# Two-branch attention: the scan or normalisation emitted one step later, PSUM copies assigned to an engine by branch, bias tiles in a pool of their own

## The chip, the cores and the metric

The kernel runs on one NeuronCore of a Trainium2 chip. Five engines have instruction queues of their own, which run in order and wait for one another on semaphores: TensorE (PE in the profile, with PEld for its weight loads), VectorE (DVE), ScalarE (ACT), GpSimd (POOL) and SyncE (SP), which here issues nearly all DMAs. TensorE writes its results to PSUM; VectorE or ScalarE copies them from there to SBUF. The metric is the device time of one execution in microseconds; the kernel before takes 1027.94 us, the median of three runs (1027.63, 1027.94, 1033.99).

## The reference

One step of a hybrid streaming encoder layer: 1024 prompt tokens and 64 sample tokens with a cache of 512, model width 1024, all in fp32. One input projection gives two attention branches of 8 heads of 64, which are gated, projected, merged, projected again and added to the input.

```python
def stick_breaking(q, k, v, q_pos, k_pos):            # branch "sb"
    z = einsum(q, k) * ATTN_SCALE
    log_keep = where(causal, log_sigmoid(-z), 0.0)
    suffix = cumsum(log_keep, reverse=True) - log_keep
    w = where(causal, exp(log_sigmoid(z) + suffix), 0.0)
    return einsum(w, v)

def band_attention(q, k, v, q_pos, k_pos, rel_bias):  # branch "cb"
    s = einsum(q, k) * ATTN_SCALE + rel_bias[clip(q_pos - k_pos)]
    return einsum(softmax(where(k_pos >= 0, s, NEG_INF)), v)
```

## The kernel before

The kernel first makes the input projection with an algorithm that saves a part of the products (up to about 500 us of the trace), then the attention (about 503 to 885 us), then the merge and the output projection. The change lies in the attention.

The attention is one loop over a list `seq` of 136 steps. A step is a branch b, a pair of heads p (four in each branch), a block of queries t and a head hd of the pair. The whole sb branch runs first, then cb. Within a pair the sample block t = 8 comes first, with both heads in one step, then t = 0 to 7 with two steps each; so a pair has 17 steps. A step has n keys: in sb n = 128(t+1), up to 1024; in cb at most 640; for t = 8, 576.

The framework is told to keep the order in which the program emits instructions (`manual_schedule`), so the order of each engine's queue is the order of the text. One pass of the loop, for step i, emits in turn:

- `qk(i)` (L1010): TensorE makes the scores z. In sb ScalarE takes two sigmoids of z, into `kp` and `be` (L1037, L1038), and POOL sets one column of `kp`. In cb VectorE adds the bias, takes the minimum as it goes (L1040), and ScalarE takes the exponential with its sum (L1044).
- `prefetch` and `load_z`: DMAs on SP for the steps and pairs to come, and `flush`, which issues the stores held back from the pass before.
- `fill`: matmuls of other work that is independent of the attention (the rest of the gate projection, then the projection of the sb branch, L781 and L881), half of the step's portion.
- `av` (L1106): when a block of queries is complete, weights times values (L1125) into one PSUM buffer `o`, and on VectorE the product with the gate (L1130), which frees that buffer.
- `tr(i-3)` (L1065): TensorE transposes the weights of the step three before (L1086), in groups of at most four blocks, into one of two PSUM buffers `pt`; each group is then copied to SBUF (L1095 on ScalarE or L1097 on VectorE). A third group can't be transposed before the first has been copied.
- `mid(i)` (L1047): in sb VectorE scans `kp` (L1054) and multiplies `be` by it (L1055). In cb VectorE takes the reciprocal of the sum (L1057) and ScalarE scales `be` (L1058). `mid` has neither matmuls nor DMAs.
- the other half of `fill`.

The copies are shared out by a counter `flip`, one count for each group. Before the change, in sb three of four go to ScalarE and every fourth to VectorE; in cb they alternate.

The bias tiles of cb, two of 128x640 and one (`bsm`) for the sample block for each pair, are loaded by `load_bias` (L1158): DMAs on SP, then two small memsets on POOL. They lie in the pool `ay`, which is opened at the first step of cb after the sb pool `axs`, with `kp` and the scan's constants, is closed; `ay` takes the space that `axs` had, and it later holds other tiles (`ot`) too. The tiles of the other cb pairs are loaded one pair ahead.

Of the kernel before, what the change touches and what calls it, by code (L numbers as in the profile page):

```python
# [8 lines left out]
F32 = mybir.dt.float32  # L9
# [23 lines left out]
def hybrid_step_kernel(ctx: ExitStack, tc: tile.TileContext, x_prompt, x_sample, c_sbk, c_sbv, c_cbk, c_cbv,  # L33
# [164 lines left out]
    with ExitStack() as ph:  # L198
# [251 lines left out]
        for i in range(nb):  # L450
            for ti, t in enumerate(TO):
# [38 lines left out]
                if ti in (3, 6) and i > 0 or ti in (5, 6) and i == 0:  # L490
                    h = 1 if ti == 6 else 0
# [37 lines left out]
                if (i, ti) in ((1, 1), (1, 5)):  # L529
                    for s in range(2):  # L530
                        h = ti // 4
# [131 lines left out]
    att = ExitStack()  # L663
# [4 lines left out]
    psZ = att.enter_context(tc.tile_pool(name="az", bufs=3, space=PS))  # L668
    psT = att.enter_context(tc.tile_pool(name="at", bufs=2, space=PS))
    psO = att.enter_context(tc.tile_pool(name="ao", bufs=1, space=PS))  # L670
    sbx = ExitStack()
    ax = sbx.enter_context(tc.tile_pool(name="axs", bufs=2))

# [10 lines left out]
    def flush(every=False):  # L684
        todo = deferred[:]
        deferred.clear()
        for n, f in todo:
            if n <= 0 or every:
                f()
            else:  # L690
                deferred.append((n - 1, f))
# [18 lines left out]
    SQ, KS, VP, BI, st, wT, zts = {}, {}, {}, {}, {}, {}, {}  # L710
# [50 lines left out]
    late = {}  # L761
# [224 lines left out]
    def fill(n):  # L986
        n += owed[0]
        owed[0] = 0
        while n > 0:
# [9 lines left out]
    seq = [(b, p, t, hd) for b in ("sb", "cb") for p in range(NPAIR) for t in [8] + list(range(8))  # L999
           for hd in range(2) if t < 8 or hd == 0]  # L1000

    def band(b, t):
        if t == 8:
            return 0, 576
        if b == "sb":
            return 0, (t + 1) * 128
        k0 = max(0, t - 4)
        return k0, (t + 1 - k0) * 128

    def qk(i):  # L1010
        b, p, t, hd = seq[i]
        key = (b, p)
        r = 128
        k0, n = band(b, t)
        hs = [(0, n)] if n <= 512 else [(0, n // 2), (n // 2, n)]
        be = am.tile([128, NP], F32, name="be", bufs=4)
        if t == 8:
            s, ks, q0 = SQ[key, 3], KS[key, 1], 0
        else:
            s, ks, q0 = SQ[key, t // 3], KS[key, 0], (t % 3) * 128  # L1020
        if b == "sb":
            kp = ax.tile([128, NP + 2], F32, name="kp", bufs=3)
            G.memset(kp[:r, n:n + 1], 0.0)
        else:
            kp = am.tile([128, 4], F32, name="sm", bufs=6)
            bt = BI[2 * p + hd] if t < 8 else BI["s", p]
            off = 0 if t == 8 else 640 - n
        for j, (x, y) in enumerate(hs):
            z = psZ.tile([128, 512], F32, name="z")
            o = k0 * 128  # L1030
            m = y - x
            parts = [(2 * h + e, h) for h in ((0, 1) if t == 8 else (hd,)) for e in range(2)]
            for e, h in parts:
                TE.matmul(z[:, :m], s[:, e, q0:q0 + 128], ks[:, h, o + x:o + y], start=e == parts[0][0],  # L1034
                          stop=e == parts[-1][0])
            if b == "sb":
                A.activation(kp[:r, x:y], z[:r, :m], AF.Sigmoid, scale=-0.125)  # L1037
                A.activation(be[:r, x:y], z[:r, :m], AF.Sigmoid, scale=0.125)  # L1038
            else:
                V.tensor_tensor_reduce(be[:r, x:y], z[:r, :m], bt[:r, off + x:off + y], 1.0,  # L1040
                                       BIG if j == 0 else kp[:r, j - 1:j], OP.add, OP.min, kp[:r, j:j + 1])
        if b == "cb":
            j = len(hs) - 1
            A.activation(be[:r, :n], be[:r, :n], AF.Exp, bias=kp[:r, j:j + 1], scale=-1.0, accum_out=kp[:r, 2:3])  # L1044
        st[i] = (be, kp)

    def mid(i):  # L1047
        b, p, t, hd = seq[i]
        r = 128
        k0, n = band(b, t)  # L1050
        be, kp = st[i]
        if b == "sb":
            im = ims[:] if t == 8 else imp[:, NP - n:NP]
            V.tensor_tensor_scan(kp[:r, n - 1::-1], kp[:r, n - 1::-1], im[:, ::-1], 0.0, op0=OP.mult, op1=OP.add)  # L1054
            V.tensor_tensor(out=be[:r, :n], in0=be[:r, :n], in1=kp[:r, 1:n + 1], op=OP.mult)  # L1055
        else:
            V.reciprocal(kp[:r, 3:4], kp[:r, 2:3])  # L1057
            A.activation(be[:r, :n], be[:r, :n], AF.Copy, scale=kp[:r, 3:4])  # L1058

    def wbase(b, j):  # L1060
        return max(0, 2 * j - 4) if b == "cb" and j < 4 else 0

    flip = [0]

    def tr(i):  # L1065
        b, p, t, hd = seq[i]
        r = 128
        k0, n = band(b, t)
        be, _ = st.pop(i)
        j = t // 2 if t < 8 else 4  # L1070
        q0 = (t % 2) * 128 if t < 8 else 0
        s0 = k0 - wbase(b, j)
        nblk = (n + 127) // 128
        groups = {}
        for kb in range(nblk):
            groups.setdefault((s0 + kb) // 4, []).append(kb)
        for g, kbs in groups.items():
            wk = (b, p, j, hd, g)
            if wk not in wT:
                wT[wk] = ak.tile([128, 4, 256], F32, name="wT", bufs=4)  # L1080
            w = wT[wk]
            pt = psT.tile([128, 4, 128], F32, name="pt")
            kr = 128
            for x, kb in enumerate(kbs):
                kr = min(128, n - kb * 128)
                TE.transpose(pt[:kr, x, :r], be[:r, kb * 128:kb * 128 + kr], ident[:r, :r])  # L1086
            m = len(kbs)
            sl = (s0 + kbs[0]) % 4
            if kr < 128:
                m -= 1  # L1090
                A.activation(w[:kr, sl + m, q0:q0 + r], pt[:kr, m, :r], AF.Copy)
            if m:
                flip[0] += 1
                if flip[0] % 2 or b == "sb" and flip[0] % 4:
                    A.activation(w[:, sl:sl + m, q0:q0 + r], pt[:, :m, :r], AF.Copy)  # L1095
                else:
                    V.tensor_copy(w[:, sl:sl + m, q0:q0 + r], pt[:, :m, :r])  # L1097


    def load_z(b, p, j):  # L1100
        zt = am.tile([128, 256], F32, name="zt", bufs=3)
        nq = 256 if j < 4 else 64
        SP.dma_start(zt[:, :nq], d_z[b][p][:, 256 * j:256 * j + nq])
        zts[b, p, j] = zt
# [51 lines left out]
            load_bias(2 * np_ + 1)  # L1156

    def load_bias(h):  # L1158
        bt = late["y"].tile([128, 640], F32, name="bias", bufs=4)
        src = d_rb[h][0:1, 127:128]  # L1160
        SP.dma_start(bt, bass.AP(tensor=src.tensor, offset=src.offset, ap=[[767, 128], [1, 640]]))
        G.memset(bt[0:64, 576:640], BIG)
        G.memset(bt[64:128, 0:64], BIG)
        BI[h] = bt
        if h % 2:
            bs = BI["s", h // 2] = late["y"].tile([128, 576], F32, name="bsm", bufs=2)
            for w in range(2):
                src = d_rb[h - 1 + w][0:1, 127:128]
                SP.dma_start(bs[64 * w:64 * w + 64], bass.AP(tensor=src.tensor, offset=src.offset,
                                                             ap=[[767, 64], [1, 576]]))  # L1170
# [16 lines left out]
    for i in range(len(seq) + LAG + 1):  # L1187
        m = 0
        if i < len(seq):
            b, p, t, hd = seq[i]  # L1190
            if b == "cb" and p == 0 and t == 8 and hd == 0:
                sbx.close()
                yst = ExitStack()
                late["y"] = yst.enter_context(tc.tile_pool(name="ay", bufs=2))
                load_bias(0)
                load_bias(1)
            qk(i)
            if hd == 0:
                if t % 2 == 1 or t == 8 and (b, p) != ("sb", 0):
                    load_z(b, p, t // 2 if t < 8 else 4)  # L1200
                prefetch(b, p, t)
            acc += amount[b] * wt[b](band(b, t)[1]) / tot[b]
            if (b, p, t) == ("cb", 0, 8):
                acc += 12
            m = int(acc) - emitted
            emitted += m
        flush()
        if i < len(seq) and seq[i][:3] == ("cb", 0, 1) and hd == 1:
            late["sb"] = True
        fill(m // 2)  # L1210
        while avq:
            av(*avq.pop(0))
        if 0 <= i - LAG < len(seq):
            tr(i - LAG)
            b, p, t, hd = seq[i - LAG]
            if t == 8 or hd == 1 and t % 2 == 1:
                avq.append((b, p, t // 2 if t < 8 else 4))
        if i < len(seq):
            mid(i)
        fill(m - m // 2)  # L1220
    flush(True)
    yst.close()
# [177 lines left out]
    for i in range(2):  # L1400
# [3 lines left out]
        for q, s in enumerate(OP_):  # L1404
# [14 lines left out]
            for c in range(2) if s != "b" else ():  # L1419
# [9 lines left out]
                p = ps[:]  # L1429
# [15 lines left out]
                if s in (3, 4, 5, 6):  # L1445
                    w, half = {3: (0, 0), 4: (1, 1), 5: (1, 0), 6: (0, 1)}[s]
                    ys.append(ys.pop(0))
                    y = ys[-1]
                    x = {3: xrs.pop((i, w, half, c)) if s == 3 else None, 4: None, 5: s1[c], 6: u2[c]}[s]
                    if s == 4:  # L1450
                        p, x = u3[c], xrs.pop((i, 1, 1, c))
# [61 lines left out]
```

## Time and profile before

| | |
|---|---|
| median of the three runs | 1027.94 us |
| the profiled execution's own time | 1032.53 us |
| its span on the page | 1030.8 us |
| PE busy over the span | 981.3 us (95%) |
| DVE, ACT, POOL busy | 636.9, 514.3, 345.9 us |
| DVE busy in the sb attention (503 to 697 us) | 164.75 of 194 us |
| ACT busy there | 126.37 of 194 us |

The profile is of one execution. A row of a window view gives its length and the busy time of each engine with its number of instructions, then the clock granted to TensorE (1.00 is full speed), the share of the DMA engines and their rate. A row of groups gives line, engine and operation, the shapes, the count, the busy time and the mean duration in ns, then the idle time just before them and what ended it. A row of waits gives who waited for whom, with total, number and longest wait in us. In a timeline a row gives start and duration, and the idle time of that engine before it in square brackets.

### The profile page before, as it was taken

The page shows a single profiled execution, that of the slowest core. Times are in us where ns is not written, and L with a number is a line of the kernel's source. Part 1 is how long each engine was busy: PE and PEld are TensorE (multiplying, and loading weights), DVE is VectorE, ACT ScalarE, POOL GpSimd, SP SyncE. Part 2 cuts the span into 40 slices and gives each one's busy share as a digit, 9 for nine tenths or more (in the row PEclk, how much of TensorE's full clock was granted, in tenths as well). Part 3 has the DMA queues.
Part 4 walks back from the last instruction along what each step waited for, and adds up shares of the span by engine and source line. Part 5 has one row for each costly group of instructions (what it writes and reads, how often), then busy time and mean ns, then how long its engine had stood idle before and what let it go on. Part 6 is the DMA issues. An engine that isn't in the chain of part 4 may idle for free.

```text
span 1030.8 us, 20364 instructions
## 1 busy us (share of the span) xinstructions
PE 981.3 (95%) x7568; PEld 925.4 (90%) x7568; DVE 636.9 (62%) x1188; ACT 514.3 (50%) x1142; POOL 345.9 (34%) x356
## 2 busy tenths in 40 slices
PE   6999999999999999999999989896899999799998
PEld 5999999999999999999987868785778887799998
DVE  5466673985545565332298969793665764489745
ACT  5534442444344333332385757574777866355320
POOL 3376662124544454442111011010201100377452
PEclk9999999999999999999999989998999999999999
DMA  7636468344663433332985556446888872773642
GB/s 240 207 133 209 164 223 300 115 125 146 185 187 119 126 113 99 92 110 87 240 213 151 150 134 164 113 125 173 236 223 239 246 220 67 233 222 100 190 124 95
DMA packets 177412, 171.04 MB, mean 166 GB/s; under 512 B 35040, under 2 KB 163168, under 8 KB 177184
## 3 DMA queue, kind: packets, MB, share of 16 engines
q1 hardware_dynamic: 168592, 161.41, 53.0%
q10 hardware_dynamic: 8720, 8.33, 2.6%
q8 instruction: 60, 0.98, 0.4%
q14 instruction: 40, 0.33, 0.1%
HBM read 110.96 MB, written 58.72 MB: 165 GB/s over the span
## 4 chain that ended last, share of the span: by engine, by line
PE 78%; DVE 9%; ACT 4%; DMA 4%; issue 2%; SPq 1%; POOL 0%; DVEq 0%; ACTq 0%
PE b L634 24%; PE acc L464 19%; PE b L1427 7%; PE o L1125 6%; PE acc L781 5%; PE b L925 5%; PE pt L1086 4%; DVE kp L1054 4%; PE z L1034 3%; PE acc L881 2%; DVE be L1055 2%; ACT be L1044 2%; DVE be L1040 1%; DVE wT L1097 1%; ACT wT L1095 1%
## 5 line engine op out<-in xcount | busy, mean ns | idle before, releaser
L1086 PE MATMUL pt<-ident,be 128*128 128x128 f32 (+1 forms) x568 | 92.8, 287 | 24.1 <-DVE wT L1097 12.7
L1086 PEld LDWEIGHTS pt<-ident,be 128*128 128x128 f32 (+1 forms) x568 | 67.8, 144 | 38.8 <-DVE wT L1097 16.2
L122 POOL TENSOR_TENSOR wlo<-wraw,whi 128x1024 fp32r<-128x1024 f32 x22 | 55.4, 2519 | 118.0 <-ACT whi L115 117.8
L1054 DVE TENSOR_TENSOR_SCAN kp<-kp,imp 128x128 f32<-128x128 f32 (+7 forms) x64 | 90.4, 1412 | 0.3 <-ACT kp L1037 0.3
L1034 PE MATMUL z<-ks,sq 128*128 128x320 f32 (+5 forms) x384 | 85.1, 328 | 0.4
L1095 ACT ACTIVATE wT<-pt 128x512 f32<-128x512 f32 (+3 forms) x125 | 58.4, 477 | 54.4 <-PE pt L1086 54.2
L1125 PE MATMUL o<-wT,vp 128*64 128x256 f32 (+1 forms) x608 | 75.9, 366 | 4.8 <-ACT wT L1095 3.0
L1125 PEld LDWEIGHTS o<-wT,vp 128*64 128x64 f32 x608 | 45.8, 140 | 34.6 <-issue 7.0
L464 PE MATMUL acc<-whi,xa 128*128 128x256 f32 x256 | 74.2, 292 | 0.0
L464 PE MATMUL acc<-wlox,xm 128*128 128x256 f32 x256 | 70.7, 278 | 0.0
L464 PE MATMUL acc<-whi,xm 128*128 128x256 f32 x256 | 70.7, 278 | 0.0
L464 PE MATMUL acc<-wlo,xa 128*128 128x256 f32 x256 | 70.6, 278 | 0.0
L464 PE MATMUL acc<-whix,xm 128*128 128x256 f32 x256 | 70.6, 278 | 0.0
L464 PE MATMUL acc<-whix,xb 128*128 128x256 f32 x256 | 70.6, 278 | 0.0
L1034 PEld LDWEIGHTS z<-ks,sq 128*128 128x128 f32 x384 | 66.8, 190 | 2.7 <-DVE sm L1040 1.7
L781 PE MATMUL acc<-xm,whi 128*128 128x384 f32 (+1 forms) x192 | 65.8, 343 | 0.0
L1055 DVE TENSOR_TENSOR be<-be,kp 128x128 f32<-128x128 f32 (+8 forms) x68 | 55.4, 815 | 9.1
L1037 ACT ACTIVATE kp<-z 128x384 f32<-128x384 f32 (+6 forms) x104 | 51.7, 497 | 15.6 <-PE z L1034 12.0
L1044 ACT ACTIVATE be<-be,sm 128x640 f32<-128x640 f32 (+5 forms) x68 | 47.4, 697 | 24.2 <-DVE sm L1040 23.4
L642 DVE TENSOR_TENSOR u<-b,s 128x256 f32<-128x256 f32 (+1 forms) x48 | 20.7, 439 | 56.2 <-PE b L634 54.9
L1038 ACT ACTIVATE be<-z 128x384 f32<-128x384 f32 (+6 forms) x104 | 52.1, 501 | 0.0
L1058 ACT ACTIVATE be<-be,sm 128x640 f32<-128x640 f32 (+5 forms) x68 | 47.4, 697 | 9.0 <-DVE sm L1057 8.6
(300 smaller groups left out, 3158.9 us busy)
## 6 DMA issues: line engine op xcount, KB each, us to landing
wraw<-in_w_in_dram SPq DMA_DIRECT2D x32, 512.0 KB, 4.6
wrawx<-in_w_in_dram SPq DMA_DIRECT2D x16, 512.0 KB, 4.4
sq<-d_qsbT SPq DMA_DIRECT2D x32, 192.0 KB, 3.6
sq<-d_qcbT SPq DMA_DIRECT2D x32, 192.0 KB, 4.0
gt<-d_gsb SPq DMA_DIRECT2D x30, 192.0 KB, 3.8
xt<-in_x_prompt_dram SPq DMA_DIRECT2D x8, 512.0 KB, 5.2
d_kcbT<-hl SPq DMA_DIRECT2D x8, 512.0 KB, 4.4
d_qcbT<-hl SPq DMA_DIRECT2D x8, 512.0 KB, 5.5
```

The lines of the kernel that those rows point to most:

```text
L122: (eng or G).tensor_tensor(out=l, in0=raw, in1=h[:].bitcast(F32), op=OP.subtract)
L464: TE.matmul(ps, x, w, start=m == 0, stop=m == len(steps) - 1)
L634: TE.matmul(ps[:, :m], w[:, hl_, k], right[s](x)[:, k, a:b], start=s < 3 and k == 0 and e == 0, stop=k == 3 and e == 2, skip_group_check=s ...
L781: TE.matmul(ps[:, :b - a], w[:, k], xk(x, k)[:, a:b], start=k == 0 and n == 0, stop=k == KT - 1 and n == 2)
L1034: TE.matmul(z[:, :m], s[:, e, q0:q0 + 128], ks[:, h, o + x:o + y], start=e == parts[0][0], stop=e == parts[-1][0])
L1044: A.activation(be[:r, :n], be[:r, :n], AF.Exp, bias=kp[:r, j:j + 1], scale=-1.0, accum_out=kp[:r, 2:3])
L1054: V.tensor_tensor_scan(kp[:r, n - 1::-1], kp[:r, n - 1::-1], im[:, ::-1], 0.0, op0=OP.mult, op1=OP.add)
L1055: V.tensor_tensor(out=be[:r, :n], in0=be[:r, :n], in1=kp[:r, 1:n + 1], op=OP.mult)
L1086: TE.transpose(pt[:kr, x, :r], be[:r, kb * 128:kb * 128 + kr], ident[:r, :r])
L1095: A.activation(w[:, sl:sl + m, q0:q0 + r], pt[:, :m, :r], AF.Copy)
L1125: TE.matmul(o[hd * 64:hd * 64 + 64, c0:c1], vv[:kr, kb, hd * 64:hd * 64 + 64], wT[b, p, j, hd, s // 4][:kr, s % 4, c0:c1] if j < 4 else wT ...
L1427: TE.matmul(ps[:, t], left[s](xs_, k)[:, ts_], wt_[:, k], start=s < 3 and t == k == e == 0, stop=k == 3 and e == 2, skip_group_check=s > 2 ...
```

## The change

Four things are altered. `mid` of a step is emitted in the following pass, right after that pass's `qk`, and so ahead of its stores, filling matmuls, `av` and `tr`. All copies of transposed blocks of sb go to ScalarE; of those of cb every fourth goes to ScalarE and the rest to VectorE. The bias tiles move to a pool `ab` that is open during the whole attention, with one buffer of `bsm` in place of two. The first pair's bias is loaded in sb's last pair, at its step t = 6, not at the first step of cb.

```diff
+    ab = att.enter_context(tc.tile_pool(name="ab", bufs=1))
...
-                if flip[0] % 2 or b == "sb" and flip[0] % 4:
+                if b == "sb" or flip[0] % 4 == 0:
                     A.activation(w[:, sl:sl + m, q0:q0 + r], pt[:, :m, :r], AF.Copy)
                 else:
                     V.tensor_copy(w[:, sl:sl + m, q0:q0 + r], pt[:, :m, :r])
...
     def load_bias(h):
-        bt = late["y"].tile([128, 640], F32, name="bias", bufs=4)
+        bt = ab.tile([128, 640], F32, name="bias", bufs=4)
...
-            bs = BI["s", h // 2] = late["y"].tile([128, 576], F32, name="bsm", bufs=2)
+            bs = BI["s", h // 2] = ab.tile([128, 576], F32, name="bsm", bufs=1)
...
                 late["y"] = yst.enter_context(tc.tile_pool(name="ay", bufs=2))
+            if (b, p, t, hd) == ("sb", 3, 6, 0):
                 load_bias(0)
                 load_bias(1)
             qk(i)
...
+        if 0 < i <= len(seq):
+            mid(i - 1)
         flush()
...
-        if i < len(seq):
-            mid(i)
         fill(m - m // 2)
```

## The prediction

> **What bounds the kernel now.** I read the busy times first, then the attention by stages, then who waits for whom there, then the places where TensorE stands still. The first two lines are the page's; under the column line come the whole sb attention, its four pairs, three stretches at half clock, and cb.
>
> ```profile
> span 1030.8 us, 20364 instructions
> PE 981.3 (95%) x7568; PEld 925.4 (90%) x7568; DVE 636.9 (62%) x1188; ACT 514.3 (50%) x1142; POOL 345.9 (34%) x356
> ...
> core 0: us, PE busy (x) PEld busy (x) DVE busy (x) ACT busy (x) POOL busy (x), PEclk, DMA share, GB/s
> 503.00:697.00 194.00, 179.24 (x1265) 153.59 (x1263) 164.75 (x178) 126.37 (x304) 20.37 (x70) 0.97 0.59 156
> 503.00:549.70 46.70, 42.77 (x302) 37.59 (x300) 40.21 (x43) 31.64 (x80) 4.51 (x18) 1.00 0.83 217
> 549.70:596.10 46.40, 43.99 (x317) 37.20 (x317) 40.38 (x47) 31.90 (x75) 3.87 (x17) 1.00 0.58 154
> 596.10:648.80 52.70, 47.40 (x328) 39.87 (x328) 43.59 (x47) 32.88 (x81) 6.79 (x20) 0.94 0.55 142
> 648.80:697.10 48.30, 45.18 (x318) 39.04 (x318) 40.68 (x46) 29.96 (x69) 5.22 (x16) 0.96 0.44 115
> 601.14:607.87 6.73, 6.73 (x34) 4.47 (x36) 1.20 (x4) 1.25 (x3) 0.20 (x2) 0.54 0.00 0
> 651.66:655.00 3.34, 3.34 (x14) 2.93 (x16) 1.20 (x4) 1.78 (x4) 0.20 (x2) 0.50 0.00 0
> 705.22:709.60 4.38, 4.38 (x21) 4.36 (x21) 0.46 (x3) 3.54 (x9) 0.00 (x0) 0.50 0.68 196
> 709.60:885.00 175.40, 167.16 (x1211) 140.45 (x1210) 104.28 (x366) 124.06 (x276) 21.75 (x25) 1.00 0.72 202
> ```
>
> TensorE bounds the whole at 95%, so a gain can only be its idle time and its slow clock. In sb it idles 194.0 - 179.2 = 14.8 us, and VectorE is nearly as full (164.75 us). The stretches at half clock follow idle gaps; they cost half their length: 3.4 and 1.7 us in sb, 2.2 us after it. The next rows are the waits of 503 to 697 us, then the groups of the copies there.
>
> ```profile
> DVE zt L1130 <- PE o L1125: 15.5, 5, 6.1
> PE pt L1086 <- DVE wT L1097: 12.0, 8, 3.2
> PE o L1125 <- DVE wT L1097: 1.1, 3, 0.7
> PE pt L1086 <- DVE be L1055: 0.8, 1, 0.8
> PE pt L1086 <- ACT wT L1095: 0.6, 1, 0.6
> ...
> L1095 ACT ACTIVATE wT<-pt 128x512 f32<-128x512 f32 (+3 forms) x71 | 34.6, 505 | 42.9 <-PE pt L1086 42.7
> L1097 DVE COPY wT<-pt 128x512 f32<-128x512 f32 (+3 forms) x23 | 12.6, 550 | 0.2
> ```
>
> Of 14.5 us that TensorE waits, 13.1 us are for the 23 copies on VectorE (0.57 us each) and 0.6 us for the 71 on ScalarE (under 0.01 us each). A copy takes about as long on either; VectorE's are late because they stand in its queue. The timeline shows one such place.
>
> ```profile
> 645.21 2.28 DVE L1054 TENSOR_TENSOR_SCAN kp<-kp,imp 128x1024 f32<-128x1024 f32 x1
> ...
> 647.62 1.23 DVE L1055 TENSOR_TENSOR be<-be,kp 128x1024 f32<-128x1024 f32 x1
> 648.16 0.60 ACT L1095 ACTIVATE wT<-pt 128x512 f32<-128x512 f32 x1 [0.65 <-PE pt L1086]
> 648.76 1.35 DVE L1054 TENSOR_TENSOR_SCAN kp<-kp,ims 128x576 f32<-128x576 f32 x1
> 650.25 0.76 DVE L1055 TENSOR_TENSOR be<-be,kp 128x576 f32<-128x576 f32 x1
> 650.92 0.68 DVE L1097 COPY wT<-pt 128x512 f32<-128x512 f32 x1
> 651.66 1.97 PE L1086 MATMUL pt<-ident,be 128*128 128x128 f32 x8 [3.20 <-DVE wT L1097]
> ```
>
> The transposes at 651.66 needed `be`, ready at 648.85, and a free `pt`. ScalarE copied its group at 648.16; VectorE's copy stood behind two scans and two products. TensorE idled 3.20 us, and its clock fell.
>
> At the start of cb the first bias load decides.
>
> ```profile
> 697.15 0.81 SPq L1161 DMA_DIRECT2D bias<-d_rb  x2
> 698.01 1.11 SPq L1169 DMA_DIRECT2D bsm<-d_rb  x2
> 702.65 0.46 DVE L1040 CUSTOM_DVE_ANT_0 be<-z,bsm 128x288 f32<-128x288 f32 x1 [5.52 <-DMA bsm<-d_rb]
> 703.82 0.77 ACT L1044 ACTIVATE be<-be,sm 128x576 f32<-128x576 f32 x1 [9.18 <-DVE sm L1040]
> 704.59 0.57 ACT L1095 ACTIVATE wT<-pt 128x512 f32<-128x512 f32 x1
> 705.22 1.97 PE L1086 MATMUL pt<-ident,be 128*128 128x128 f32 x8 [7.89 <-ACT wT L1095]
> ```
>
> The load starts at 697.15, just as the last product of sb ends (697.13), because its tiles take the space of `kp`. VectorE waits for it, the exponential for VectorE, a copy of transposes stands behind the exponential, and TensorE loses 7.89 us plus the 2.2 us of clock.
>
> **The change part by part.** *`mid` one pass later.* In sb `qk` has no VectorE work, so VectorE's order stays scan, product, `av` product, next scan: nothing changes, and I cost it at nothing. It issues no DMA, so SP's order is untouched, and TensorE's as well. The filling work that it is moved past has evictions on ScalarE and, late in cb, products on VectorE; `be` has two more passes before its transposes, and they are the cover. Without it a pass waits for the reciprocal and scaling, under 1 us by the cb rows below.
>
> *Copies in sb.* Twenty-three copies, 12.6 us, leave VectorE, and ScalarE gets them at 505 ns: 126.4 + 11.6 = 138 of some 179 us. At the rate of the rows above 94 copies on ScalarE cost TensorE 0.8 us where both engines cost 13.7. What is late next is the scan. VectorE's pairs without copies are 37 to 40 us (40.21 to 43.59 less 3.15), and 2 us of gaps between scan and product (0.13 us each, 647.49 to 647.62); TensorE's pairs at full clock are 42.8, 44.0, 44.0 (47.40 - 3.4) and 43.5 (45.18 - 1.7). TensorE is the longer by 1 to 4 us, least in the third pair. I leave 1 us of waiting for scans in each pair, 4 us in all; the bounds are 0.8 us (the row for `be`) and 12 us (3 us in every pair, as at 651.66). The clock comes back, 5.1 us. Gain: 14.5 + 5.1 - 4 = 15.6 us.
>
> [...]
>
> *Bias in its own pool.* The tiles overlap nothing that is in use, and two bias loads and two of `bsm` are issued some 20 us early on SP, ahead of a query load that is needed only in cb. They land in under 5 us (`bsm` issued from 698.01, VectorE released at 702.65). The POOL memsets wait for it, and the `kp` memset of t = 6 is behind them; its reader is the product a pass or more later, so at most 2 us, taken as 0. The 7.89 us go, but what follows is a chain of its own: after the scores of cb's first step VectorE does that reduction (702.65 to 703.78, 1.1 us), the last scan and product (3.6 us, as 645.21 to 648.85), the next reduction (0.4 us); ScalarE an exponential (0.6 us), a scaling (0.8) and a copy (0.6). That is 7.1 us. TensorE's own work up to the transposes that need that copy is about 5.3 us: 3.5 us to where it stopped at 697.34, 1.0 of transposes, 0.8 of fill. So 2 us stay. Gain: 7.9 + 2.2 - 2 = 8.1 us; bounds 2 and 10.1 us.
>
> [...]
>
> ```profile
> 601.14 1.12 PE L1086 MATMUL pt<-ident,be 128*128 128x128 f32 x4 [2.76 <-DVE wT L1097]
> ```
>
> [...]
>
> *Copies in cb.* These are the groups of 705 to 885 us, then TensorE's waits from 706 us on.
>
> ```profile
> L1097 DVE COPY wT<-pt 128x512 f32<-128x512 f32 (+3 forms) x51 | 25.5, 500 | 7.6 <-PE pt L1086 6.8
> L1095 ACT ACTIVATE wT<-pt 128x512 f32<-128x512 f32 (+3 forms) x54 | 23.8, 441 | 11.5 <-PE pt L1086 11.5
> L1057 DVE RECIPROCAL sm<-sm 128x1 f32<-128x1 f32 x67 | 10.7, 160 | 26.0 <-ACT be L1044 25.1
> ...
> PE o L1125 <- ACT wT L1095: 3.0, 5, 1.8
> PE pt L1086 <- ACT wT L1095: 1.8, 6, 0.4
> PE pt L1086 <- DVE wT L1097: 0.8, 2, 0.4
> PE o L1125 <- DVE wT L1097: 0.7, 1, 0.7
> ```
>
> About 25 copies of 0.5 us go to VectorE: 104 + 12.5 = 117 of 175 us. The reciprocal no longer makes VectorE wait 25 us for the exponential, so there is room. TensorE's 4.8 us behind ScalarE's copies halve; the 1.5 us behind VectorE's grow by half: 4.8 - 2.4 - 0.75, a gain of about 1.5 us, bounds -14 (25 copies at sb's 0.57 us) and 4.8.
>
> Sum: 15.6 + 8.1 + 1.5 = 25.2 us. The profiled execution took 1032.53 us (span 1030.8), so 1007.3; it is 4.6 us above the median 1027.94, from which 1002.7 comes. Whether those 4.6 us are waits that go anyway I can't tell, and take the middle, 1005 us.
>
> **The rivals.** *B, the scan takes the copy's place:* VectorE still ends last in sb, and only its 12.6 us of copies go, the clock stays low: 12.6 + 8.1 + 1.5 = 22.2, about 1008 us. For it: VectorE's 164.75 us. Against: it waited 15.5 us of sb for TensorE's `o`.
>
> *C, ScalarE alone is too slow in sb:* each moved copy holds TensorE as the single ScalarE wait of 0.6 us does: 23 x 0.6 = 14 us back, about 1019 us. For it: a copy stands behind four sigmoids. Against: 71 copies cost 0.6 us.
>
> *D, slower:* in cb the copies on VectorE queue behind reductions as sb's did behind scans. 76 x 0.57 = 43 us less the 1.5 of now: about 1046 us. It decides above (1038 - 1005)/76 = 0.43 us a copy; now it is 1.5/51 = 0.03.
>
> *E, the boundary's chain* takes the whole 7.9 us though the load is early (another transfer or the table load of ScalarE in it): the 8.1 us are lost, about 1013 us. For it: the 7.1 us chain. Against: its start is earlier.
>
> **How the numbers follow.** My forecast has 0.60, B 0.15, C 0.14, D 0.06, E 0.05. Only C (within) and D (slower) are not faster by over 1%, which is about what a measurement of this kernel can tell from no change: faster 0.80, same 0.14, slower 0.06. The low end takes all of TensorE's idle time and lost clock from 503 to 885 us: 14.8 + 7.9 + 8.2 + 7.3 = 38 us from the profiled time, 995 us. The high end is C, rounded up to 1020 us.
>
> **What would show it.** Right: no copy of VectorE in sb; TensorE's wait there under 5 us, its releaser the product (L1055); no stretch at half clock in the pairs; at the start of cb no wait for `bsm` and under 3 us of idle. Wrong: waits of transposes for ScalarE's copies in sb above 10 us (C), TensorE waiting for VectorE's copies in cb above 30 us (D), pairs still above 46 us with the product as releaser (B).

## The result, and the profile after

The changed kernel takes 999.82 us (median of four runs, 998.98 to 1001.83) beside 1029.77 us for the kernel before (four runs, with one of 1031.60 us beside the three above); the ratio is 0.9707, with a 95% interval of 0.9668 to 0.9746. The profiled execution took 1000.43 us against 1032.53 us. These are the first lines of its page. The run with the late load below had one execution of 1585.48 us at a granted clock of 0.56, which its ratio leaves out.

```profile
span 998.6 us, 20448 instructions
## 1 busy us (share of the span) xinstructions
PE 966.4 (97%) x7568; PEld 917.9 (92%) x7568; DVE 631.9 (63%) x1188; ACT 510.0 (51%) x1142; POOL 346.6 (35%) x356
```

The work is the same and TensorE is busy for 97% of a shorter span. To see where the 32.2 us of span went, I cut both traces at the same events: TensorE's first scores of a pair (the eight matmuls of its sample block). The rows of the window view are, for the kernel before, all of sb, then cb's first pair (called the boundary below), then cb's second and third pairs.

```profile
505.39:692.65 187.26, 172.50 (x1216) 146.86 (x1214) 160.53 (x175) 124.57 (x302) 20.37 (x70) 0.97 0.60 157
692.65:747.52 54.87, 44.07 (x312) 37.93 (x311) 28.74 (x90) 34.37 (x77) 6.86 (x12) 0.91 0.70 194
747.52:827.52 80.00, 76.82 (x567) 64.73 (x565) 50.93 (x188) 61.65 (x140) 8.67 (x13) 1.00 0.86 236
```

The same three stretches of the changed kernel:

```profile
505.53:672.77 167.24, 164.29 (x1216) 143.68 (x1214) 149.90 (x152) 132.30 (x325) 22.69 (x74) 1.00 0.70 187
672.77:717.57 44.80, 41.01 (x311) 35.49 (x311) 27.05 (x93) 33.42 (x74) 5.89 (x8) 1.00 0.65 187
717.57:795.30 77.73, 74.16 (x567) 63.48 (x565) 55.33 (x201) 54.76 (x126) 8.69 (x13) 1.00 0.86 241
```

The stretches give 20.0, 10.1 and 2.3 us; what comes after takes 203.3 us in both (1030.8 - 827.5 and 998.6 - 795.3). In sb TensorE's idle time (length less the first busy figure) falls from 14.8 to 3.0 us and its busy time by 8.2 us with the same 1216 matmuls. About 4.8 us of these are the two stretches at half clock, which are gone (6.73 us at 0.54 and 3.34 us at 0.50 of the clock lose 3.1 and 1.7 us; the granted clock of all sb was 0.97 and is now 1.00). VectorE's 23 copies are gone (175 instructions, now 152), and ScalarE has them.

These are the waits of the changed kernel in sb (503 to 672 us).

```profile
PEld o L1126 <- ACT wT L1096: 2.2, 7, 0.5
PE pt L1087 <- DVE be L1056: 2.1, 3, 0.8
PE pt L1087 <- ACT wT L1096: 0.7, 1, 0.7
```

Ninety-four copies on ScalarE hold TensorE's matmuls for 0.7 us, and what is late next is VectorE's product, with 2.1 us. The start of cb, in the timeline of the changed kernel:

```profile
673.50 0.46 DVE L1041 CUSTOM_DVE_ANT_0 be<-z,bsm 128x288 f32<-128x288 f32 x1
...
674.55 2.28 DVE L1055 TENSOR_TENSOR_SCAN kp<-kp,imp 128x1024 f32<-128x1024 f32 x1
...
674.77 0.78 ACT L1045 ACTIVATE be<-be,sm 128x576 f32<-128x576 f32 x1
...
675.62 0.98 ACT L1096 ACTIVATE wT<-pt 128x512 f32<-128x512 f32 x2
...
679.50 1.06 ACT L1096 ACTIVATE wT<-pt 128x512 f32<-128x512 f32 x2
680.13 1.14 PE L1087 MATMUL pt<-ident,be 128*128 128x128 f32 x8 [1.28 <-ACT wT L1096]
```

The reduction starts at 673.50 with its bias long there (the two loads of `bsm` are issued from 657.41 us, and the trace's eight take 3.7 to 4.8 us to land). The last scan of sb stands behind it, ScalarE's exponential and copies follow at once, and TensorE idles 1.28 us in place of 7.89 us. The full clock stays (1.00 in the boundary's row above).

### The profile page after: what moved, and what is told of

It reads as the page before. It is cut to its first block, busy times and chain, and to the rows that moved or that the text cites. A ratio compares the mean times of both kernels' runs of the same rounds, so it can differ in the third digit from the quotient of the medians.

```text
span 998.6 us, 20448 instructions
## 1 busy us (share of the span) xinstructions
PE 966.4 (97%) x7568; PEld 917.9 (92%) x7568; DVE 631.9 (63%) x1188; ACT 510.0 (51%) x1142; POOL 346.6 (35%) x356
## 4 chain that ended last, share of the span: by engine, by line
PE 84%; ACT 5%; DVE 4%; DMA 3%; issue 2%; SPq 1%; POOL 1%; DVEq 0%; ACTq 0%
PE b L634 25%; PE acc L464 19%; PE b L1429 8%; PE o L1126 6%; PE acc L782 6%; PE pt L1087 5%; PE b L926 5%; PE z L1035 5%; PE acc L882 2%; DVE be L1041 1%; ACT be L1059 1%; ACT be L1045 1%; ACT wT L1096 1%; DMA wrawx<-in_w_in_dram 1%; PE pk L349 1%
## 5 line engine op out<-in xcount | busy, mean ns | idle before, releaser
L1087 PE MATMUL pt<-ident,be 128*128 128x128 f32 (+1 forms) x568 | 88.5, 278 | 10.0 <-ACT wT L1096 6.9
L1055 DVE TENSOR_TENSOR_SCAN kp<-kp,imp 128x128 f32<-128x128 f32 (+7 forms) x64 | 88.3, 1379 | 0.6 <-ACT kp L1038 0.6
L1087 PEld LDWEIGHTS pt<-ident,be 128*128 128x128 f32 (+1 forms) x568 | 65.5, 140 | 23.0 <-ACT wT L1096 11.0
L1126 PE MATMUL o<-wT,vp 128*64 128x256 f32 (+1 forms) x608 | 68.5, 357 | 2.0 <-ACT wT L1096 1.0
L1126 PEld LDWEIGHTS o<-wT,vp 128*64 128x64 f32 x608 | 42.7, 136 | 27.2 <-issue 5.9
L1045 ACT ACTIVATE be<-be,sm 128x640 f32<-128x640 f32 (+5 forms) x68 | 47.4, 697 | 35.4 <-DVE sm L1041 34.8
L1056 DVE TENSOR_TENSOR be<-be,kp 128x128 f32<-128x128 f32 (+8 forms) x68 | 57.3, 843 | 9.4 <-ACT sg L757 0.5
L1038 ACT ACTIVATE kp<-z 128x384 f32<-128x384 f32 (+6 forms) x104 | 52.2, 502 | 10.1 <-PE z L1035 4.5
L464 PEld LDWEIGHTS acc<-whi,xa 128*128 128x128 f32 x256 | 47.9, 188 | 0.1
```

What stands on the lines that cost most here:

```text
L464: TE.matmul(ps, x, w, start=m == 0, stop=m == len(steps) - 1)
L1126: TE.matmul(o[hd * 64:hd * 64 + 64, c0:c1], vv[:kr, kb, hd * 64:hd * 64 + 64], wT[b, p, j, hd, s // 4][:kr, s % 4, c0:c1] if j < 4 else wT ...
```

## The experiments

Each run has its edit against the changed kernel or against the kernel before. The table gives the ratio to the kernel before on the same chip with its 95% interval, and the same three stretches of the profiled execution (by the timelines, from the first scores of a pair to those of the next) in us. The last pair and the tail are not in it. The profiled execution of the result has 44.8 us at the boundary where the control has 45.4: the control lost some 1.7 us there to slow clock (from 708.98 to about 712.5 us its matmuls of 128x384 take 0.52 us, where they take 0.33 to 0.42 us before), so a difference of 1 us at the boundary between two executions says little.

| run | ratio (95%) | sb | boundary | cb pairs 2, 3 |
|---|---|---|---|---|
| kernel before | 1 | 187.3 | 54.9 | 80.0 |
| changed kernel, again | 0.972 (0.9698 to 0.9742) | 167.0 | 45.4 | 77.7 |
| sb copies undone | 0.9931 (0.9905 to 0.9957) | 185.9 | 46.1 | 77.7 |
| `mid` undone | 0.9747 (0.9719 to 0.9774) | 166.9 | 48.7 | 78.2 |
| cb copies undone | 0.9743 (0.9718 to 0.9768) | 166.9 | 46.0 | 80.7 |
| late load, own pool | 0.9716 (0.969 to 0.9743) | 167.6 | 45.6 | 77.8 |
| only sb copies | 0.9829 (0.9808 to 0.985) | 166.9 | 54.9 | 80.0 |
| only bias pool | 0.9942 (0.9924 to 0.996) | 185.5 | 48.6 | 80.0 |
| extra VectorE work | 0.9859 (0.9837 to 0.988) | 177.2 | 49.4 | 77.8 |
| half of it | 0.9803 (0.978 to 0.9826) | 172.9 | 48.0 | 77.8 |
| `mid` late once only | 0.9737 (0.9715 to 0.9759) | 167.5 | 45.2 | 77.8 |
| all cb copies on VectorE | 0.9717 (0.969 to 0.9743) | 166.9 | 42.3 | 83.4 |
| low parts on VectorE | 0.9727 (0.9704 to 0.975) | 166.6 | 44.8 | 77.8 |

**The control.** The changed kernel ran once more beside the others.

> The changed kernel itself, as the measure for the runs beside it: 0.971 of the kernel before, about 1000 us.

It came to 0.972, 1001.97 us.

**The copies of sb, undone and alone.** Undone:

```diff
-                if b == "sb" or flip[0] % 4 == 0:
+                if flip[0] % 4 == 0 if b == "cb" else flip[0] % 4:
```

> The changed kernel with one part undone: in sb every fourth copy is on VectorE again. If those copies are what held TensorE in sb (the queue theory), most of the sb gain is lost: the changed kernel's 1000 us becomes 1015 to 1020, and TensorE waits in sb some 13 us for VectorE's copies, as in the kernel before. If the move of the scan (mid) is what frees TensorE, the time stays within 3 us of 1000.

Alone, in the kernel before:

```diff
-                if flip[0] % 2 or b == "sb" and flip[0] % 4:
+                if b == "sb" or flip[0] % 2:
```

> The kernel before with one part alone: all copies of sb on ScalarE, everything else as before. The queue theory: the whole sb gain comes with it, 20 us as the pair starts of the changed kernel show, so 1010 us (ratio about 0.981); the wait for bsm at the start of cb stays. If the gain needs the other parts, less than 12 us are gained.

Undone, the time is 1023.96 us, more than the 1015 to 1020 us expected, and sb takes 185.9 us although `mid` is at its new place. Alone, sb takes 166.9 us, as with the whole change, and the boundary keeps its 54.9 us. So the sb gain is that of the copies, all of it. The time of that run, 1014.12 us, is 17.6 us less by its ratio and not the 20 us that I had expected from the stretch; its interval reaches from 15.5 to 19.8 us. These are TensorE's waits in sb (503 to 680 us) with the copies undone:

```profile
PE pt L1087 <- DVE wT L1098: 11.9, 8, 3.2
PE o L1126 <- DVE wT L1098: 1.2, 3, 0.7
```

They are those of the kernel before, to 0.1 us.

**Position in the queue, or load on the engine.** Both explain these runs: a copy on VectorE stands behind scans, and it takes VectorE's time. This kernel puts the time back and not the wait. In sb, where every fourth copy stood, VectorE makes a product of the same size that nobody reads; the real copy stays on ScalarE.

```diff
+    scr = ab.tile([128, 4, 128], F32, name="scr", bufs=1)
...
+                if b == "sb" and flip[0] % 4 == 0:
+                    A.activation(w[:, sl:sl + m, q0:q0 + r], pt[:, :m, :r], AF.Copy)
+                    one = ident[:, None, :].to_broadcast([128, m, 128])
+                    V.tensor_tensor(out=scr[:, :m], in0=one, in1=one, op=OP.mult)
```

> The changed kernel with extra work on VectorE: where every fourth copy of sb had stood, VectorE makes a product of a constant of the same size (about 0.6 us each, 23 in sb) into a tile that nobody reads; the real copy stays on ScalarE. If the copies held TensorE by standing behind scans while TensorE waited for them (the queue theory), the extra work costs at most 5 us, as TensorE's pairs are the longer. If it was VectorE's load as such, most of the 20 us of sb are lost again (1012 us or above).

The second has it only where `flip[0] % 8 == 0`.

> As the run with extra VectorE work in sb, but half as many (about 12 products, 7 us in all, 1.7 us in a pair). If VectorE has a slack of 1 to 4 us in each pair, as the prediction reckoned, these cost at most 2 us beside the changed kernel; if it has none, about half of what the full set costs, 7 us.

The queue theory's bounds, 5 and 2 us, were both passed: 1016.37 and 1011.99 us. The full set takes 10.2 us more than the control in sb and 3.9 us at the boundary, the half set 5.9 and 2.6 us. But "most of the 20 us of sb", as the load theory had it, did not come back either. TensorE's waits in sb are, with the full set and then with the half set:

```profile
PE pt L1088 <- DVE be L1057: 8.8, 4, 2.9
PE pt L1088 <- ACT wT L1101: 0.7, 1, 0.7
```

```profile
PE pt L1088 <- DVE be L1057: 6.2, 4, 1.9
PE pt L1088 <- ACT wT L1102: 0.7, 1, 0.7
```

Nobody waits for the extra products; TensorE waits for the scan's product (L1057), 8.8 and 6.2 us where the changed kernel has 2.1. The rest is clock, as these stretches after two of the waits show, the first of the full set, the second of the half set (4.24 us at 0.62 and 4.12 us at 0.59 of the clock lose 1.6 and 1.7 us). The full set has a second such loss, after a wait of 2.44 us, so 6.7 us of waits and some 3.4 us of clock (0.98 granted over its 503 to 686 us) make its 10.2 us. In that second loss the 32 matmuls of weights and values from 551.24 us take 4.99 us, where those of the half set at the same place take 3.46.

```profile
597.76:602.00 4.24, 4.24 (x24) 2.96 (x26) 3.74 (x7) 2.19 (x6) 0.25 (x4) 0.62 0.24 79
```

```profile
594.88:599.00 4.12, 4.12 (x22) 3.26 (x24) 3.72 (x7) 2.30 (x6) 0.21 (x3) 0.59 0.32 103
```

So of the 18.9 us that sb loses with the real copies (185.9 less the control's 167.0), about 10 us come with VectorE's time alone (the 23 products take 12.7 us, the 23 copies of the kernel before 12.6). The other 9 us come on top when TensorE waits for a copy behind a scan. This is a difference of two runs: with the products ScalarE still has all 94 copies, which it has not when they are undone. Neither theory alone is right. The extra work costs nothing in sb's first pair (37.05 us from 505.59 to 542.64, beside 37.04). The later pairs take 47.2, 47.4 and 45.6 us where the changed kernel has 43.8, 43.2 and 43.2; the waits for the product grow by 1.7, 2.6 and 2.4 us in them, for 2.9, 3.4 and 3.9 us of extra products, and the first two lose 1.7 us of clock each besides.

**`mid` undone, and late once.** In the first kernel `mid(i)` is back behind `tr`; in the second only the last step of sb keeps the new place.

```diff
-        if 0 < i <= len(seq):
-            mid(i - 1)
+        if i == 68:
+            mid(67)
...
+        if i < len(seq) and i != 67:
+            mid(i)
         fill(m - m // 2)
```

> The changed kernel with mid back at its old place, copies and bias pool as changed. The queue theory: VectorE's order in sb is the same with either place, so sb does not change, and the whole stays within 3 us of 1000 us. If the move of mid is a cause of its own, 5 to 15 us are lost.

> The changed kernel with mid at its old place in all steps but the last one of sb, whose scan is emitted after cb's first reduction. If the move of mid is worth its 4 us only there (the scan of 3.6 us no longer ahead of the reduction that ScalarE's copies stand behind), the time is that of the changed kernel within 1.5 us. If it also helps within cb, it stays 3 us or more above.

Undone, sb does not change (166.9 us), and the boundary takes 48.7 us instead of 44.8 (the control: 45.4). The timeline there:

```profile
673.10 2.28 DVE L1055 TENSOR_TENSOR_SCAN kp<-kp,imp 128x1024 f32<-128x1024 f32 x1
...
676.66 0.45 DVE L1041 CUSTOM_DVE_ANT_0 be<-z,bsm 128x288 f32<-128x288 f32 x1
...
677.82 0.77 ACT L1045 ACTIVATE be<-be,sm 128x576 f32<-128x576 f32 x1 [3.27 <-DVE sm L1041]
...
678.60 0.96 ACT L1096 ACTIVATE wT<-pt 128x512 f32<-128x512 f32 x2
...
679.22 1.09 PE L1087 MATMUL pt<-ident,be 128*128 128x128 f32 x8 [1.98 <-ACT wT L1096]
...
681.14 1.97 PE L1087 MATMUL pt<-ident,be 128*128 128x128 f32 x8
```

The scan and product of 3.6 us stand ahead of the reduction, ScalarE's copies stand behind the exponential that waits for it, TensorE idles 1.98 us, and soon after the same eight transposes take 1.97 us in place of 1.09. With only this one `mid` late the boundary takes 45.2 us. The times (1005.66 and 1004.04 us) are 3.7 and 2.1 us above the control's median, for `mid` undone between the two outcomes that I had named; their intervals overlap the control's, so they don't tell these apart. The stretches do it, each in one execution.

**The bias load late, and the pool alone.** The first kernel loads at the first step of cb again but into the own pool; the second is the kernel before with the own pool and the early load.

```diff
-            if (b, p, t, hd) == ("sb", 3, 6, 0):
+            if (b, p, t, hd) == ("cb", 0, 8, 0):
                 load_bias(0)
                 load_bias(1)
```

> The changed kernel with the bias pool of its own, but the first load emitted at the first step of cb, as before. If the wait came from the space that the tiles shared with kp, SP issues the load some 5 us before the first reduction and the time stays within 2 us of 1000. If the earlier place in the program is what matters, the wait for bsm comes back with 5 to 8 us and the time is 1005 to 1010 us.

> The kernel before with one part alone: the bias pool of its own with the early first load. Nothing changes in sb; the idle 7.9 us and the 2.2 us of slow clock at the start of cb go, but the last scan of sb still stands ahead of cb's first reduction (3.6 us). So 5 to 7 us are gained, about 1024 us; 8 to 10 us if the order there does not matter; under 2 us if another wait takes the whole place.

The late load costs nothing (1002.61 us, boundary 45.6; its two loads of `bsm` are issued from 667.16 us, the reduction starts at 673.89 us and waits for no DMA): what held it was the shared space, not the place in the program. The pool alone gives 0.9942, 6 us, with 6.2 us at the boundary, where the last scan still stands ahead of the reduction.

**The copies of cb.** First alternating again (`if b == "sb" or flip[0] % 2`), then all on VectorE (`if b == "sb"`).

> The changed kernel with cb's copies alternating again between ScalarE and VectorE. My term for cb's copies was 1.5 us, so 1001 to 1002 us; if the shift to VectorE is worth more than that, 1004 us or above; if it costs time (VectorE's copies behind reductions), below 999 us.

> The changed kernel with all of cb's copies on VectorE. TensorE's 6 to 7 us of waits in cb are now for the fourth copies on ScalarE, which stand behind an exponential that waits for VectorE's reduction. If that place is the cause, they go: 996 to 999 us where the changed kernel takes 1000. If VectorE's copies queue behind reductions as rival D has it, 25 more of them cost 0.43 us or more each: 1010 us or above.

Alternating costs 1.2 us at the boundary (beside 44.8 us; neither execution has slow clock there: 1.00 in the row above, and with the copies alternating the filling matmuls take 0.42 us at most, where the control's slow ones take 0.52) and 3.0 us in the next two pairs, by the stretches; the time, 1004.96 us, agrees, but its interval overlaps the control's. All on VectorE gains 2.6 us at the boundary and loses 5.7 us later; in all the time, 1001.74 us, is the same, which rules out rival D's rate and my hope as well. TensorE then waits for VectorE's copies (672 to 835 us):

```profile
PE pt L1087 <- DVE wT L1098: 5.6, 5, 3.3
```

**The low parts of the weights on VectorE.**

```diff
-                            W.split(("u", j + 1) if j + 1 < len(units) else ("p", 0))
+                            W.split(("u", j + 1) if j + 1 < len(units) else ("p", 0), None if "y" in late else V)
```

> The changed kernel with the low part of the weights of the filling matmuls made by VectorE, not by POOL, during sb. In the trace of the changed kernel four or five of VectorE's scans and products in sb take 2 us longer while POOL makes such a part. If VectorE's time is what sets sb, each 2 us collision is replaced by 1.2 us of its own work: 2 to 4 us gained. If TensorE sets sb with slack on VectorE, the time stays the same; if VectorE then waits for ScalarE's high part, it is longer.

No change (1002.94 us, sb 166.6 us). It tests less than I meant. In these groups of VectorE (503 to 672 us) the products (L1056) are shorter, 50.4 us where the changed kernel has 56.1, and the scans by 4 us in all, but the new work (6.1 us) and its wait for ScalarE (3.4 us) take back what the collisions had cost. In the changed kernel five of these instructions took about 2 us longer than others of their size, each while POOL made a low part; these are a product of the usual length, the low part on POOL, and a product of the same size beside it.

```profile
517.97 0.69 DVE L1056 TENSOR_TENSOR be<-be,kp 128x512 f32<-128x512 f32 x1
...
519.69 3.02 POOL L122 TENSOR_TENSOR wlo<-wraw,whi 128x1024 fp32r<-128x1024 f32 x1 [4.39 <-ACT whi L115]
...
520.65 2.62 DVE L1056 TENSOR_TENSOR be<-be,kp 128x512 f32<-128x512 f32 x1
```

The groups with the low parts on VectorE:

```profile
L1056 DVE TENSOR_TENSOR be<-be,kp 128x128 f32<-128x128 f32 (+8 forms) x67 | 50.4, 752 | 8.9
L122 DVE TENSOR_TENSOR wlo<-wraw,whi 128x1024 fp32r<-128x1024 f32 x5 | 6.1, 1223 | 3.4 <-ACT whi L115 3.4
```

None of these kernels beats the changed one.

## Why the prediction was right, and where it was not

The time, 999.82 us, lies in the range and somewhat below the 1005 us; against the profiled execution the sum was 25.2 us and the spans give 32.2 us. All three terms were too small, by 4.4, 2.0 and 0.8 us.

*Copies in sb: right mechanism, term too small.* 15.6 us were predicted, 20.0 us measured. The waits for copies went as told, ScalarE's cost stayed under 1 us, and the half clock went. Three sizes were off. The rest left for scans was 4 us and is 2.1 us plus 0.7 us of ScalarE. The clock was taken at half for the whole 6.73 us, though its row has 0.54: 5.1 us, and 4.8 by the rows. And I took TensorE's loss from its idle time alone; its busy time fell by 8.2 us, 3.4 us more than the clock explains. The weight loads had shown it: in the kernel before they waited longer than the matmuls. These are their waits of 503 to 697 us.

```profile
PEld pt L1086 <- DVE wT L1097: 14.1, 9, 3.3
PEld o L1125 <- DVE wT L1097: 3.3, 6, 1.1
```

That is 17.4 us against the 13.1 us of the matmul rows. Over all the engines that they wait for, the waits of the weight loads in sb fell from 21.3 to 6.0 us, and these 15.3 us with the 4.8 us of clock make up the 20.0 us; the waits of the matmuls fell by 11.7 us only. The matmuls' ends are modelled, so a wait can lie within a busy time; that the 3.4 us are this is argued from the rows (the matmuls of weights and values, which read the copies, fell from 36.1 to 32.0 us) and not shown by a run.

*The reason behind that term was half wrong.* The step that failed is "TensorE is the longer by 1 to 4 us": I compared sums over a pair (by the prediction's own figures 1.6 to 4.8 us) and gave VectorE a slack. The extra products show that it has nearly none in the later pairs. A sum over a pair leaves out that the engines wait for each other at a pair's start. Two rows of the run with the full set of products, whose second pair starts at 542.64 us, show it: TensorE's transposes wait for the last product of the pair before, and soon after VectorE waits for TensorE's `o`.

```profile
549.56 1.06 PE L1088 MATMUL pt<-ident,be 128*128 128x128 f32 x8 [2.44 <-DVE be L1057]
556.28 0.42 DVE L1136 TENSOR_TENSOR zt<-o,zt 128x256 f32<-128x256 f32 x1 [1.98 <-PE o L1131]
```

Rival B had this: the product did become the releaser. Its price was wrong, since both engines came out of the copies' way and the clock came back.

*Bias pool: the waits went as told, but the term was not the pool's alone.* 8.1 us with 2 us left were predicted; 10.1 us came in the stretch, with 1.28 us left, and the pool alone gives 6.2 us of them. The predicted chain (reduction, last scan, next reduction, exponential, scaling, copy) is the one in the timeline.

*`mid` one pass later: cost at nothing, and wrong at one place.* In sb it is nothing, as told. But the chain at the boundary was drawn up with the last scan already behind the reduction, so 3 to 4 us of that term belong to the move of `mid` (48.7 us undone, 45.2 us with one late step), and about 6 us to the pool.

*Copies in cb: the size nearly right, by luck.* 1.5 us were predicted, 2.3 us measured in the two pairs of the table. But the term halved the waits behind ScalarE's copies, and these did not fall: in the two pairs matmuls wait 1.9 us for them before and 2.4 us after, and 0.7 and 0.8 us for VectorE's. What fell is TensorE's busy time, from 76.82 to 74.16 us with the same 567 matmuls at full clock (the rows above). The matmuls of weights and values took 17.8 us before, 15.9 us after and 17.7 us with the copies of cb undone, so the gain is the copies', and most of it lies there; why is not shown.

*The clock:* the 4.8 us of sb came back. The gaps of 2.76 and 3.20 us ahead of the two stretches at half clock (the rows of 601.14 and 651.66 in the prediction) went with the copies, and the longest wait of TensorE's matmuls in sb is now 0.8 us. *Rival C* fell: all 94 copies on ScalarE hold TensorE's matmuls for 0.7 us, and 23 of them back on VectorE cost 18.9 us in sb; in the kernel before VectorE was busy for 164.75 of 194 us there.

The timed parts add up: only sb copies 17.6 us, only the pool 6.0 us, and what undoing adds to the control, `mid` 2.8 us and cb copies 2.4 us, make 28.8 us; the control gained 28.9 us (0.028 of 1031.82). Each part has an interval of about 2 us either way or more, so that they meet so closely is luck.

## What to carry to other kernels

Before a copy goes to the engine with free time on average, look at what stands ahead of it in that engine's queue: a copy that TensorE waits for does not belong behind work that is itself late, and here 23 of 94 copies cost 20 us, about half of them for their place in the queue and half for the engine's time. The slack of an engine that another waits for is not safely read from sums of busy time (here they gave 1.6 to 4.8 us a pair, and 12.7 us of products that nobody read cost 10.2 us of sb); put extra work on one, without a consumer, and see whether the time grows. And where a phase ends, look for loads held back by shared space (7.89 us of idle here) and for the old phase's last piece ahead of the new phase's first (3.6 us of scan and product).

## What the runs showed of the hardware that was not expected

TensorE's clock fell after shorter gaps than those of the kernel before (2.76, 3.20 and 7.89 us), and the gap's length does not decide alone. Two gaps of the run with half the extra products are of one length. These are the matmuls that end them, and the stretch after the first.

```profile
548.99 1.07 PE L1088 MATMUL pt<-ident,be 128*128 128x128 f32 x8 [1.92 <-DVE be L1057]
...
594.88 1.66 PE L1088 MATMUL pt<-ident,be 128*128 128x128 f32 x8 [1.93 <-DVE be L1057]
```

```profile
549.00:594.00 45.00, 43.17 (x317) 37.11 (x317) 40.48 (x42) 34.47 (x84) 6.30 (x18) 1.00 0.60 163
```

The gap of 1.92 us was followed by 1.00 of the clock, the one of 1.93 us by 0.59 (the row of 594.88 above), with the same eight transposes in 1.66 us in place of 1.07. With the full set of extra products a gap of 2.60 us was followed by 0.62 of the clock (the row of 597.76 above), and one of 2.94 us, which ends at 644.63, by none lost.

```profile
644.63 1.07 PE L1088 MATMUL pt<-ident,be 128*128 128x128 f32 x8 [2.94 <-DVE be L1057]
```

```profile
644.63:649.00 4.37, 4.37 (x38) 3.32 (x40) 3.74 (x7) 2.14 (x6) 0.31 (x4) 1.00 0.13 38
```

With `mid` undone, a gap of 1.98 us that ends at 679.22 was followed by full clock up to 680.30 and by half clock soon after; in the changed kernel the gap of 1.28 us ahead of 680.13 by full clock.

```profile
679.22:680.30 1.08, 1.08 (x9) 1.08 (x10) 0.00 (x0) 1.08 (x3) 0.00 (x0) 1.00 0.13 45
680.30:681.20 0.90, 0.87 (x6) 0.53 (x5) 0.44 (x3) 0.90 (x4) 0.00 (x0) 0.55 0.00 0
681.20:682.00 0.80, 0.80 (x4) 0.80 (x5) 0.00 (x0) 0.80 (x3) 0.00 (x0) 0.50 0.04 10
```

So of two gaps of one length one cost 1.7 us of clock and the other nothing. What decides besides the length these runs do not show.
